# A hybrid decoder layer: input scales ahead of the pairs, the second pair's projections before the first pair's output, one-hots from bias columns

## The chip, the cores and the metric

The kernel runs on one core of one Trainium2 chip. The metric is device time in microseconds for one launch, the median of three runs. One execution was profiled; its rows are in a section below.

## The reference, cut to what matters

One layer on 1024 tokens of width 1024, in float32:

```python
h = x
h = h + _token_mixers(_rmsnorm(h, norm_mix), ...)     # attention heads and a conv module, then W_out
h = h + _peer(_rmsnorm(h, norm_ffn), ...)             # product-key retrieval over 128 * 128 experts
ple_gate = sigmoid(_rmsnorm(h, norm_ple) @ w_ple_gate)
h = h + ple_gate * (p @ w_ple_proj)
return _rmsnorm(h, final_norm)
```

`_rmsnorm` divides each token's row by the root of its mean square. The mixer projects the normed row to q, k, v and two conv inputs, runs three dilated causal windows over earlier tokens and a causal depthwise conv of 31 taps, and projects both through `w_out`. `_peer` finds for each token and each of 8 heads the 16 best of 128 * 128 experts, as pairs of the best 16 in two lists of 128 keys; an expert is one row of `expert_u` and one of `expert_v`: gelu(x . u) times a gate, times v.

## The kernel before, in words

The 1024 tokens are 8 tiles of 128, taken in four pairs (`GROUPS`; pair 0 holds tiles 0 and 1). Each pair passes through stages: `stage_in` (L823: load x, norm, transpose, projections q, k, v), `stage_attend` (L827: attention of the two tiles, then `convolve`), `stage_out` (L832: norms of both halves, `w_out`, residual, norm for the experts), `stage_search` (L837: queries, scores, the best 16 per list), `stage_combine` (L840: the best 16 pairs, indices and gates). Below, in(1) is `stage_in` of pair 1, and so on. Attention of a pair needs keys and values of the pairs before.

The experts are computed in two ways. For tiles 0, 1, 6, 7 (`FEW`) each of the 128 chosen rows of a token is fetched: `gather_all` (L623) walks these tiles one after the other, per tile 128 fetches of `expert_u` (GpSimd issues an indirect DMA, L592, for one slot of 128 tokens, 512 KB) each with a product and sum on VectorE (L605), then 128 fetches of `expert_v` with a multiply-add on VectorE (L621): 1024 fetches in all. For tiles 2 to 5 (`ALL`) all experts are computed: `gate_matrix` (L633) writes a matrix of gates per token and expert to DRAM, and `dense` (L697) streams both tables past it on TensorE, in split precision (lines L733 to L735 and L764 to L766). A closing stage `embed` (L772) follows for every tile.

A framework puts the instructions in order when the kernel is built: it walks them with estimated costs, and on each engine the ready instruction that was emitted first goes next; `tc.high_priority()` lifts a block. The order on each engine is then fixed, and an instruction at the head of a queue that waits holds up all that is behind it. The fetches are emitted last. SyncE (SP) issues the plain loads, in an order fixed in the same way. Tiles with the same tag share a few buffers: `xn` (2: x of a pair, later normed rows), `t4` (2: attention scores, large temporaries of `combine`), `w` (3 weight pieces), `xT` (1).

Norm scales come from `rstd` (L140): a square with row sum on ScalarE per tile, a square root on ScalarE (L150), a reciprocal on VectorE (L152). `normed_input` (L281) calls it, rescales the rows in place on ScalarE (L285) and transposes them on TensorE (L161, `pt_mix`).

The conv runs 16 of its taps on ScalarE and GpSimd (L348, L349) and 15 on VectorE (L355); `cc` at L356 joins them.

`gate_matrix` works through groups of four slots, 32 per tile. For each it needs two one-hot matrices of 128 lines, one scaled by the gate (`oa`, VectorE, from `less_keys` of `i1`: two matmuls into `pd` that give index minus key), one plain (`o2`). Every second group makes `o2` on VectorE by a comparison (L668). The others make it on ScalarE from a second `less_keys` (L674, L675): 1 - |index - key|, cut at 0. Four products then fill `pG` (L678), and ScalarE copies it out (L679).

Of the kernel before, what the change touches and what calls it, by code (L numbers as in the profile page):

```python
# [10 lines left out]
F32 = mybir.dt.float32  # L11
# [4 lines left out]
AF = mybir.ActivationFunctionType  # L16
# [4 lines left out]
P = 128  # L21
D = 1024
# [3 lines left out]
GROUPS = ((0, 1), (2, 3), (4, 5), (6, 7))  # L26
NG = len(GROUPS)
# [74 lines left out]
def tile_layer(ctx, tc, t, consts, out):  # L102
    nc = tc.nc
    V, S, G = nc.vector, nc.scalar, nc.gpsimd

    x_d = t["x"][0]
# [10 lines left out]
    rows = lambda i: slice(i * P, (i + 1) * P)  # L117
    half = lambda f: slice(f * 512, (f + 1) * 512)

    def scope(parent, **kw):  # L120
        s = parent.enter_context(ExitStack())
        return s, s.enter_context(tc.tile_pool(bufs=1, **kw))

    cpool = ctx.enter_context(tc.tile_pool(name="cpool", bufs=1))
    small = ctx.enter_context(tc.tile_pool(name="small", bufs=2))
# [4 lines left out]
    mix, mpool = scope(ctx, name="mpool")  # L130
# [6 lines left out]
    acc = bank(ps_keep, "acc", 1)  # L137


    def rstd(srcs, n, name, junk=None, pool=small):  # L140

        ssq = pool.tile([P, len(srcs)], F32, tag="ssq", name=f"ssq_{name}", bufs=2)
        for j, src in enumerate(srcs):
            sq = junk(f"sqj_{name}_{j}") if junk else mpool.tile([P, D], BF16, tag="t2", name=f"sqj_{name}_{j}", bufs=3)
            S.activation(sq[:, :n], src, AF.Square, accum_out=ssq[:, j : j + 1])
        return inv_sqrt(ssq, 1.0 / n, name, pool)

    def inv_sqrt(v, scale, name, pool=small):
        sd = pool.tile([P, v.shape[1]], F32, tag="sd", name=f"sd_{name}", bufs=2)
        S.activation(sd, v, AF.Sqrt, bias=eps, scale=scale)  # L150
        r = pool.tile([P, v.shape[1]], F32, tag="r", name=f"r_{name}", bufs=4)
        V.reciprocal(r, sd)  # L152
        return r

    def transpose_to(dst, src, n, name, ps_tile, gain=None):

        for b in range(0, n, 4):
            m = min(4, n - b)
            pt = ps_tile(f"pt_{name}_{b}")
            for i in range(m):  # L160
                nc.tensor.transpose(pt[:, rows(i)], src[:, rows(b + i)], ident)  # L161
            if gain is None:
                S.copy(dst[:, b : b + m, :], pt[:, : m * P].rearrange("p (m c) -> p m c", c=P))
            else:
                for i in range(m):
                    S.activation(dst[:, b + i, :], pt[:, rows(i)], AF.Copy, scale=gain[:, b + i : b + i + 1])
# [5 lines left out]
    ident, iota = col(C_ID, P), col(C_IOTA, P)  # L172
# [12 lines left out]
    bias = apool.tile([P, SEQ], F32, name="bias")  # L185
# [87 lines left out]
    def load(g):  # L273
        xs = []
        for i in GROUPS[g]:
            xt = mpool.tile([P, D], F32, tag="xn", name=f"xt{i}", bufs=2)
            nc.sync.dma_start(xt, x_d[rows(i), :])
            xs.append(xt)
        return xs

    def normed_input(g, xs):  # L281
        r = rstd(xs, D, f"mix{g}")
        xT = apool.tile([P, KD, GN], F32, tag="xT", name=f"xT{g}")[:, :, : len(xs) * P]
        for j in range(len(xs)):
            S.activation(xs[j], xs[j], AF.Copy, scale=r[:, j : j + 1])  # L285
            transpose_to(xT[:, :, rows(j)], xs[j], KD, f"mix{g}_{j}", tps, g_mix)
        return xT

# [12 lines left out]
    def qkv(g, xT):  # L301
        qT = apool.tile([P, GT, H // 2, P], F32, tag="qT", name=f"qT{g}", bufs=2)

        def done_k(j, a):
            i = GROUPS[g][j]
            k = apool.tile([P, DA], F32, tag="qk", name=f"k{i}")
            S.copy(k, a)
            rope(k, i)
            transpose_to(kT[:, :, rows(i)], k, H // 2, f"k{i}", tps)

        def done_q(j, a):
            i = GROUPS[g][j]
            q = apool.tile([P, DA], F32, tag="qk", name=f"q{i}")
            S.copy(q, a)
            rope(q, i)
            transpose_to(qT[:, j], q, H // 2, f"q{i}", tps)

        token_major(xT, w_qkv, 1, f"k{g}", done_k)
        token_major(xT, w_qkv, 0, f"q{g}", done_q)
        token_major(xT, w_qkv, 2, f"v{g}", lambda j, a: S.copy(vt[:, GROUPS[g][j], :], a))  # L320
        return qT
# [82 lines left out]
    def mixed(g, ys, cT):  # L404
# [13 lines left out]
        for j in range(nt):  # L418
# [5 lines left out]
            V.bn_aggr(mv[:, j, :], st)  # L424
            pcs.append(pc)
        r = inv_sqrt(mv[:, :, 1], 1.0, f"ln{g}")
        yc = []
        for j in range(nt):
# [204 lines left out]
    def gate_matrix(gp, j, i1, i2, gate):  # L633

        tr = []
        for what, src in (("i2", i2), ("g", gate)):
            f = flat(src)
            if what != "g":
                f32 = mpool.tile([P, SLOTS], F32, tag="t2", name=f"gl{what}{j}", bufs=3)
                S.copy(f32, f)  # L640
                f = f32
            pt = pps(f"pgt{what}{j}")
            nc.tensor.transpose(pt[:, 0:P], f, ident)
            d = gp.tile([P, P], F32, tag=f"{what}T", name=f"{what}T{j}", bufs=2)
            S.copy(d, pt[:, 0:P])
            tr.append(d)
        i2T, gT = tr
        four = [P, 4, NK]

        def less_keys(ix, t0, name):  # L650

            pd = lin(name).rearrange("p (t k) -> p t k", k=NK)
            nc.tensor.matmul(pd, flat(ix), ident16[:, t0 : t0 + 4].unsqueeze(2).to_broadcast(four), start=True, stop=False)
            nc.tensor.matmul(pd, ones16, minus16.to_broadcast([1, 4, NK]), start=False, stop=True)
            return pd

        for b in range(P // BT):
            stage = gp.tile([P, NK, BT], F32, tag="stage", name=f"stage{j}_{b}", bufs=2)
            for o in range(0, BT, 4):
                t0 = b * BT + o  # L660
                oa = gp.tile(four, F32, tag="oa", name=f"oa{j}_{t0}", bufs=2)
                V.scalar_tensor_tensor(
                    oa, less_keys(i1, t0, f"pd1_{j}_{t0}"), 0.0, gT[:, t0 : t0 + 4].unsqueeze(2).to_broadcast(four),
                    ALU.is_equal, ALU.mult,
                )
                o2 = gp.tile(four, F32, tag="o2", name=f"o2_{j}_{t0}", bufs=3)
                if o % 8 == 0:
                    V.tensor_tensor(  # L668
                        o2, i2T[:, t0 : t0 + 4].unsqueeze(2).to_broadcast(four),
                        iota.unsqueeze(1).to_broadcast(four), ALU.is_equal,  # L670
                    )
                else:

                    S.activation(o2, less_keys(i2, t0, f"pd2_{j}_{t0}"), AF.Abs)  # L674
                    S.activation(o2, o2, AF.Relu, bias=1.0, scale=-1.0)  # L675
                pg = sps(f"pG{j}_{t0}")
                for e in range(4):
                    nc.tensor.matmul(pg[:, rows(e)], o2[:, e, :], oa[:, e, :], start=True, stop=True)  # L678
                S.copy(stage[:, :, o : o + 4], pg.rearrange("p (t i) -> p i t", i=NK))  # L679
            nc.sync.dma_start(gd[j, :, :, b], stage.rearrange("p (q c) t -> p q (c t)", c=GROUP))  # L680
# [137 lines left out]
    xs = load(0)  # L818
    load_tables()
    fetched, wide, h1s = {}, {}, {}  # L820
    st = {}

    def stage_in(g):  # L823
        xT = normed_input(g, xs if g == 0 else load(g))
        st[g] = (qkv(g, xT), xT)

    def stage_attend(g):  # L827
        qT, xT = st[g]
        ys = attend(g, qT)
        st[g] = (ys, convolve(g, xT))  # L830

    def stage_out(g):  # L832
        yT = mixed(g, *st[g])
        h1s[g] = project(g, yT)
        st[g] = normed_ffn(g, h1s[g])

    def stage_search(g):  # L837
        st[g] = search(g, st[g])

    def stage_combine(g):  # L840
        vals, idxs = st[g]
        for j, i in enumerate(GROUPS[g]):
            if i in FEW:
                i1, i2, gate = combine(i, vals[j], idxs[j], gpool, NF)
                fetched[i] = (places(i, i1, i2), gate)
            else:
                wide[i] = combine(i, vals[j], idxs[j], mpool, ND)

    stage_in(0)
    stage_attend(0)  # L850
    for g in range(NG - 1):
        if g > 0:
            stage_in(g + 1)
        stage_out(g)
        stage_search(g)
        if g == 0:
            stage_in(g + 1)
        if g > 0:
            stage_attend(g + 1)
        stage_combine(g)  # L860
        if g == 0:
            stage_attend(g + 1)
# [5 lines left out]
    gph, gp = scope(ctx, name="gph", side="right")  # L868
# [10 lines left out]
    for j, i in enumerate(ALL):  # L879
        gate_matrix(gp, j, *wide[i])  # L880
# [91 lines left out]
```

## Time and profile before

| | us |
|---|---|
| median of three runs (3216.42 to 3229.95) | 3220.88 |
| profiled execution | 3223.85 |
| its span, first to last instruction | 3222.1 |
| TensorE busy in the span | 2791.2 (87%) |
| VectorE busy | 2604.3 (81%) |
| ScalarE busy | 1098.6 (34%) |
| GpSimd busy | 1535.3 (48%) |

All times in the rows are microseconds from the first instruction. PE is TensorE's matmul, PEld its weight load, DVE VectorE, ACT ScalarE, POOL GpSimd. A matmul's end in the trace is modelled, and matmuls are pipelined, so that their times overlap. L12 is line 12 of the kernel. The granted clock is the share of TensorE's full speed that it was given.

### The profile page before, as it was taken

To read this page: it belongs to the slowest core of one execution; us is meant where nothing else is said; L and a number is where in the kernel's file an instruction comes from. 1 tells how busy PE (TensorE), PEld (TensorE's weight loads), DVE (VectorE), ACT (ScalarE), POOL (GpSimd) and SP (SyncE) were. 2 spreads that over 40 slices of the span, in tenths; PEclk is the share of its full clock that TensorE was granted. 3 is DMA by queue.
4 is the path that set the end of the run, shared out by engine and by line. 5 is a ranking of instruction groups with operands and counts; after the bars stand their busy time and mean duration, and the time that the engine had idled before them with its cause. 6 is when DMAs were issued, how large, how long until landed. Compare 5 with 4: busy or idle time off the path is not lost. (4 is left out here: it accounts for less than half of the span.)

```text
span 3222.1 us, 36302 instructions
## 1 busy us (share of the span) xinstructions
PE 2791.2 (87%) x11839; PEld 2020.0 (63%) x11839; DVE 2604.3 (81%) x5147; ACT 1098.6 (34%) x1926; POOL 1535.3 (48%) x1268
## 2 busy tenths in 40 slices
PE   6688959958995859995999998999999989999998
PEld 3464625843673536663777775777777757777764
DVE  1728886997899898885888887888889878888974
ACT  2712543363245126663222223222222322232233
POOL 0501585455435512324555555565566555555651
PEclk9898978979997879998999999999999999999999
DMA  5154769718932937989999999999999999999982
GB/s 161 53 176 160 264 208 335 260 46 314 338 140 94 347 126 225 291 266 368 329 338 328 327 324 345 329 339 347 320 338 331 322 339 338 335 331 330 325 316 101
DMA packets 307984, 878.36 MB, mean 273 GB/s; under 512 B 27162, under 2 KB 94130, under 8 KB 307794
## 3 DMA queue, kind: packets, MB, share of 16 engines
q0 software_dynamic: 147456, 536.94, 46.2%
q1 hardware_dynamic: 157072, 335.74, 30.1%
q10 hardware_dynamic: 3266, 3.36, 0.3%
q8 instruction: 93, 1.52, 0.2%
q14 instruction: 97, 0.79, 0.1%
HBM read 833.99 MB, written 41.94 MB: 272 GB/s over the span
## 5 line engine op out<-in xcount | busy, mean ns | idle before, releaser
L592 POOL DMA_INDIRECT u<-in_expert_u_dram,ex x512 | 657.0, 1283 | 888.6 <-DVE hk L605 547.0
L592 POOL DMA_INDIRECT v<-in_expert_v_dram,ex x512 | 683.1, 1334 | 546.9 <-DVE gy L621 405.8
L621 DVE SCALAR_TENSOR_TENSOR gy<-v,ga,gy 128x1024 f32<-128x1024 f32 x512 | 656.8, 1283 | 58.7 <-DMA v<-in_expert_v_dram,ex 50.3
L605 DVE CUSTOM_DVE_ANT_0 u<-u,gxn 128x1024 f32<-128x1024 f32 x512 | 616.4, 1232 | 36.5 <-DMA u<-in_expert_u_dram,ex 36.3
L735 PE MATMUL ph<-xh,ul 128*128 128x512 f32 x1024 | 411.1, 401 | 37.7 <-DVE ul L711 37.6
L734 PE MATMUL ph<-xl,uh 128*128 128x512 f32 x1024 | 408.8, 399 | 0.0
L733 PE MATMUL ph<-xh,uh 128*128 128x512 f32 x1024 | 408.2, 399 | 0.4 <-ACT gelu L737 0.2
L751 ACT CAST vh<-v 128x1024 fp32r<-128x1024 f32 x128 | 131.3, 1050 | 675.4 <-PE py L766 476.7
L764 PE MATMUL py<-vh,ah 128*128 128x512 f32 x640 | 255.1, 399 | 38.4 <-ACT ah L743 38.3
L349 POOL TENSOR_TENSOR side<-side,tap 128x256 f32<-128x256 f32 x240 | 195.0, 814 | 183.7 <-ACT tap L348 169.8
L735 PEld LDWEIGHTS ph<-xh,ul 128*128 128x128 f32 x1024 | 196.3, 192 | 91.8 <-DVE ul L711 48.9
L766 PE MATMUL py<-vh,al 128*128 128x512 f32 x640 | 251.2, 397 | 0.3 <-DVE al L745 0.3
L765 PE MATMUL py<-vl,ah 128*128 128x512 f32 x640 | 249.9, 394 | 0.0
L753 DVE TENSOR_TENSOR vl<-v,vh 128x1024 fp32r<-128x1024 f32 x128 | 155.5, 1220 | 108.7 <-ACT vh L751 105.4
L269 PE MATMUL pq<-x2T,w_pq 128*128 128x256 f32 x1024 | 231.4, 384 | 4.0 <-DMA w_pq<-in_peer_wq_dram 3.0
L733 PEld LDWEIGHTS ph<-xh,uh 128*128 128x128 f32 x1024 | 196.7, 192 | 45.2 <-ACT gelu L737 2.4
L734 PEld LDWEIGHTS ph<-xl,uh 128*128 128x128 f32 x1024 | 196.5, 192 | 44.5 <-issue 2.2
L269 PEld LDWEIGHTS pq<-x2T,w_pq 128*128 128x128 f32 x1024 | 194.6, 193 | 32.9 <-ACT pqT L479 4.5
L709 ACT CAST uh<-u 128x1024 fp32r<-128x1024 f32 x128 | 134.3, 1049 | 127.3 <-PE ph L734 84.2
L743 ACT CAST ah<-gelu 128x512 fp32r<-128x512 f32 x128 | 79.3, 619 | 274.7 <-DVE gelu L741 272.3
L711 DVE TENSOR_TENSOR ul<-u,uh 128x1024 fp32r<-128x1024 f32 x128 | 156.0, 1219 | 20.8 <-DMA gt<-gate_d 13.3
L764 PEld LDWEIGHTS py<-vh,ah 128*128 128x128 f32 x640 | 120.8, 189 | 76.1 <-ACT ah L743 50.2
(265 smaller groups left out, 4939.2 us busy)
## 6 DMA issues: line engine op xcount, KB each, us to landing
u<-in_uT_dram SPq DMA_DIRECT2D x128, 512.0 KB
v<-in_expert_v_dram SPq DMA_DIRECT2D x128, 512.0 KB
w_pq<-in_peer_wq_dram SPq DMA_DIRECT2D x64, 512.0 KB
gate_d<-stage SPq DMA_DIRECT2D x16, 2048.0 KB
gt<-gate_d SPq DMA_DIRECT2D x64, 512.0 KB
w_o<-in_w_out_dram SPq DMA_DIRECT2D x32, 512.0 KB
we<-in_w_ple_gate_dram SPq DMA_DIRECT2D x24, 512.0 KB
w_k<-in_w_qkv_dram SPq DMA_DIRECT2D x16, 512.0 KB
```

Of the source, the lines that this page charges most:

```text
L269: nc.tensor.matmul(a, w[:, k, :], xT[:, k, :], start=k == 0, stop=k == KD - 1)
L349: G.tensor_tensor(side, side, m, ALU.add)
L592: d = G.indirect_dma_start(out=e, out_offset=None, in_=table, in_offset=bass.IndirectOffsetOnAxis(ap=index, axis=0))
L605: uses(V.tensor_tensor_reduce(out=e, in0=e, in1=xn, scale=1.0, scalar=0.0, op0=ALU.mult, op1=ALU.add, accum_out=hk[:, k : k + 1]))
L621: uses(V.scalar_tensor_tensor(y, e, act[:, k : k + 1], y, ALU.mult, ALU.add))
L711: V.tensor_tensor(lo, u, hi.bitcast(F32), ALU.subtract)
L733: nc.tensor.matmul(ph, hi, xh[:, k, :], start=k == 0, stop=False)
L734: nc.tensor.matmul(ph, hi, xl[:, k, :], start=False, stop=False)
L735: nc.tensor.matmul(ph, lo, xh[:, k, :], start=False, stop=k == KD - 1)
L764: nc.tensor.matmul(py, ah[e][:, rows(j)], vh[e][:, half(f)], start=first, stop=False)
L765: nc.tensor.matmul(py, ah[e][:, rows(j)], vl[e][:, half(f)], start=False, stop=False)
L766: nc.tensor.matmul(py, al[e][:, rows(j)], vh[e][:, half(f)], start=False, stop=last_e)
```

## The change

Three edits. The scales of all pairs are worked out ahead (`input_scales`): those of pair 0 first, those of pairs 1 to 3 behind `stage_attend(0)` in `later_scales`, which loads x once more, into `t4` buffers, two tiles at a time. `normed_input` only rescales. Then in(1) is emitted ahead of out(0) and search(0) instead of behind them; the later pairs had that order already. Last, the groups of `gate_matrix` that make `o2` on ScalarE no longer use `less_keys`: ScalarE takes the absolute value of the key numbers with the negated index as a bias column, four slots in four instructions; `i2N` holds the negated indices of a tile.

```diff
-        return inv_sqrt(ssq, 1.0 / n, name, pool)
+        return inv_sqrt(ssq, 1.0 / n, name, pool, r_tag)
...
+    def input_scales(g, xs):
+        r = rstd(xs, D, f"mix{g}", r_tag="r_mix")
+        for j, i in enumerate(GROUPS[g]):
+            r_mix[i] = r[:, j : j + 1]
+
+    def later_scales():
+        for g in range(1, NG):
+            xs = []
+            for i in GROUPS[g]:
+                xt = mpool.tile([P, D], F32, tag="t4", name=f"xq{i}", bufs=2)
+                nc.sync.dma_start(xt, x_d[rows(i), :])
+                xs.append(xt)
+            input_scales(g, xs)
...
     def normed_input(g, xs):
-        r = rstd(xs, D, f"mix{g}")
...
-            S.activation(xs[j], xs[j], AF.Copy, scale=r[:, j : j + 1])
+            S.activation(xs[j], xs[j], AF.Copy, scale=r_mix[GROUPS[g][j]])
...
+        i2N = gp.tile([P, P], F32, tag="i2N", name=f"i2N{j}", bufs=2)
+        S.activation(i2N, i2T, AF.Copy, scale=-1.0)
...
-                    S.activation(o2, less_keys(i2, t0, f"pd2_{j}_{t0}"), AF.Abs)
+                    for e in range(4):
+                        S.activation(o2[:, e, :], iota, AF.Abs, bias=i2N[:, t0 + e : t0 + e + 1])
                     S.activation(o2, o2, AF.Relu, bias=1.0, scale=-1.0)
...
+    input_scales(0, xs)
     stage_in(0)
     stage_attend(0)
+    later_scales()
     for g in range(NG - 1):
-        if g > 0:
-            stage_in(g + 1)
+        stage_in(g + 1)
         stage_out(g)
         stage_search(g)
-        if g == 0:
-            stage_in(g + 1)
         if g > 0:
             stage_attend(g + 1)
         stage_combine(g)
```

## Rows read from the trace of the kernel before

**Rows 1.** Stretches: length; PE, PEld, DVE, ACT, POOL busy (count); clock; DMA share; GB/s.

```profile
298.00:489.00 191.00, 147.56 (x531) 83.58 (x530) 166.42 (x365) 78.24 (x168) 128.64 (x125) 0.87 0.71 242
...
1196.00:1460.00 264.00, 252.30 (x1436) 158.72 (x1436) 221.50 (x361) 154.10 (x274) 69.88 (x65) 0.97 0.81 253
...
1440.00:1520.00 80.00, 48.15 (x175) 28.44 (x175) 45.70 (x75) 23.07 (x39) 34.18 (x28) 0.83 0.99 358
...
1491.00:3107.00 1616.00, 1500.04 (x6287) 1189.88 (x6286) 1373.20 (x1807) 442.57 (x582) 912.17 (x667) 0.98 0.92 332
3107.00:3222.00 115.00, 98.61 (x290) 48.90 (x288) 62.14 (x69) 40.56 (x90) 30.04 (x26) 0.95 0.48 181
```

**Rows 2.** The same for the gathers of line L592 alone: POOL busy (x).

```profile
298.00:489.00 191.00, 79.30 (x65) 0.87 0.71 242
```

**Rows 3.** Timeline of the tail: start, us, engine, line, operation [idle before, releaser].

```profile
3146.26 1.02 POOL L592 DMA_INDIRECT v<-in_expert_v_dram,ex  x1 [0.30 <-issue]
...
3159.22 2.60 DVE L621 SCALAR_TENSOR_TENSOR gy<-v,ga,gy 128x1024 f32<-128x1024 f32 x2
...
3209.25 2.74 PE L804 MATMUL plp<-wt,pTt 128*128 128x512 f32 x6
```

**Rows 4.** Timeline: the first matmul of the dense product, and its last.

```profile
1491.16 0.79 PE L733 MATMUL ph<-xh,uh 128*128 128x512 f32 x1
...
3107.01 0.39 PE L766 MATMUL py<-vh,al 128*128 128x512 f32 x1
```

**Rows 5.** Timeline of PE: the first transposes of pairs 1, 2 and 3.

```profile
275.76 1.11 PE L161 MATMUL pt_mix<-cst,xt 128*128 128x128 f32 x4 [9.56 <-ACT xt L285]
...
424.71 1.12 PE L161 MATMUL pt_mix<-cst,xt 128*128 128x128 f32 x4 [28.37 <-ACT xt L285]
...
722.57 1.12 PE L161 MATMUL pt_mix<-cst,xt 128*128 128x128 f32 x4 [35.72 <-ACT xt L285]
```

**Rows 6.** Pair 2's root and reciprocal; both gaps per stretch.

```profile
409.37 0.29 ACT L150 ACTIVATE sd_mix<-ssq_mix,eps 128x2 f32<-128x2 f32 x1
...
423.32 0.15 DVE L152 RECIPROCAL r_mix<-sd_mix 128x2 f32<-128x2 f32 x1
...
396.00:424.60 28.60, 0.34 (x2) 0.00 (x0) 28.60 (x49) 17.54 (x38) 19.33 (x24) 0.59 0.11 37
...
687.00:722.50 35.50, 0.00 (x0) 0.00 (x0) 35.50 (x56) 19.11 (x40) 19.72 (x25) 0.56 0.04 15
```

**Rows 7.** Around the moved stage: a stretch, then timeline of pairs 1 and 2.

```profile
121.00:201.00 80.00, 45.63 (x104) 20.60 (x105) 37.97 (x61) 35.95 (x79) 25.25 (x33) 0.74 0.28 93
...
331.00 0.38 DVE L549 TENSOR_TENSOR i<-eq 128x128 bf16<-128x128 bf16 x1
...
332.52 0.92 PE L374 MATMUL s<-kT,qT 64*128 64x384 f32 x4
...
373.57 0.89 ACT L348 ACTIVATE tap<-glu,cw 128x256 f32<-128x256 f32 x2
...
471.97 0.41 DVE L356 TENSOR_TENSOR cc<-cc,side 128x256 f32<-128x256 f32 x1
...
489.28 1.04 PE L421 MATMUL pc<-cst,cc 128*128 128x128 f32 x8
...
715.11 0.41 DVE L356 TENSOR_TENSOR cc<-cc,side 128x256 f32<-128x256 f32 x1
```

**Rows 8.** Gate matrices: two `pd` matmuls; small ScalarE operations elsewhere; the `Abs`.

```profile
1228.09 0.38 PE L653 MATMUL pd<-ident,i 128*128 128x512 bf16 x1
1228.40 0.38 PE L654 MATMUL pd<-minus,ones 1*128 1x512 bf16 x1
...
36.02 1.15 ACT L166 ACTIVATE xT<-pt_mix,gains 128x128 f32<-128x128 f32 x4 [1.01 <-PE pt_mix L161]
...
77.31 0.40 ACT L384 ACTIVATE sb<-sb,nm 128x128 f32<-128x128 f32 x1
...
L674 ACT ACTIVATE o<-pd 128x512 f32<-128x512 f32 x64 | 38.3, 598 | 17.1 <-PE pd L654 16.4 <-DVE o L668 0.7
```

More of the change, by code (lines that the diff above doesn't have):

```diff
@@ L137, in tile_layer, with rstd @@
     acc = bank(ps_keep, "acc", 1)
-    def rstd(srcs, n, name, junk=None, pool=small):
+    def rstd(srcs, n, name, junk=None, pool=small, r_tag="r"):
         ssq = pool.tile([P, len(srcs)], F32, tag="ssq", name=f"ssq_{name}", bufs=2)
@@ L145, in rstd, with inv_sqrt @@
             S.activation(sq[:, :n], src, AF.Square, accum_out=ssq[:, j : j + 1])
-        return inv_sqrt(ssq, 1.0 / n, name, pool)
-    def inv_sqrt(v, scale, name, pool=small):
+        return inv_sqrt(ssq, 1.0 / n, name, pool, r_tag)
+    def inv_sqrt(v, scale, name, pool=small, r_tag="r"):
         sd = pool.tile([P, v.shape[1]], F32, tag="sd", name=f"sd_{name}", bufs=2)
         S.activation(sd, v, AF.Sqrt, bias=eps, scale=scale)
-        r = pool.tile([P, v.shape[1]], F32, tag="r", name=f"r_{name}", bufs=4)
+        r = pool.tile([P, v.shape[1]], F32, tag=r_tag, name=f"r_{name}", bufs=4)
         V.reciprocal(r, sd)
@@ L820, in tile_layer @@
     fetched, wide, h1s = {}, {}, {}
-    st = {}
+    st, r_mix = {}, {}
     def stage_in(g):
```

## The prediction

> **What bounds the kernel now.** I read the stage table first (busy time of each engine in chosen stretches), because no engine is the bound all the way. Between 1491 and 3107 us (first `ph` to last `py` matmul [rows 4]) TensorE works on the dense experts: 1500 of 1616 us busy, DMA share 0.92 at 332 GB/s [rows 1]. This stretch is not touched by the diff and I let it keep its length. Then 115 us of tail follow [rows 1]. Second view: the same table for the row gathers of GpSimd (`fetch`, L592). Of 1024 rows 65 are issued in 298 to 489 us [rows 2]. Beside the dense product and in the tail GpSimd does nothing else, so its counts in the stage table are rows too: 667 and 26 [rows 1]; 331 lie before. A row goes out every 1616/667 = 2.42 us beside the dense product, every 1.32 us behind it (1.02 of issue and 0.30 to the next [rows 3]). The last row is added at 3161.8 us, 54.8 us behind the last `py` [rows 3, 4].
>
> So two things set the end together. The dense product must start early, and the gathers must be through. They are emitted last, so they only fill the free slots of VectorE and GpSimd; a shorter front leaves them fewer. Third view: TensorE's order of work ahead of 1491, for its idle times and what ended them; there the change acts.
>
> **How an edit moves the end.** If the dense product starts D us earlier and L rows fewer are issued before it, the dense product ends at 3107 - D, the tail of TensorE at 3107 - D + 115. The gathers end at 3107 - D + 54.8 + 1.35 L (1.32 us of spacing, a little for VectorE's own tail work). Behind the last row its tile still needs about 37 us: 5 for the norm, 21 for TensorE (transposes, two halves of 8.6), 11 from the last `plp` (at 3211) to the end [rows 3]. So end = 3107 - D + max(115, 92 + 1.35 L); up to 17 lost rows cost nothing, later ones 1.35 us each. The price of a row has 2.42 us as its upper end (dense pace to the finish) and 0 as its lower (it finds another free slot); I take 1.35, since lost rows run after the last `py`, where that pace is measured.
>
> **Scales first.** Today `stage_in` of pairs 2 and 3 starts with two squares, a square root, a reciprocal on VectorE, a rescale. TensorE waits 28.4 us before the first `pt_mix` of pair 2, 35.7 before that of pair 3, 9.6 before that of pair 1 [rows 5]. The wait isn't the arithmetic: for pair 2 the root is done at 409.7 and its reciprocal, 0.15 us long, runs at 423.3, behind convolution work in VectorE's queue [rows 6]. With scales worked out during pair 0 this wait goes; the rows of x are in their buffers by then, so the rescale on ScalarE is late next, a few us. The granted clock averages 0.59 and 0.56 over the two gaps [rows 6], near the lower of its two levels; what an earlier return to the upper one saves I count as nothing. What isn't gained: VectorE is busy 28.6 of 28.6 and 35.5 of 35.5 us in the two gaps [rows 6]. If `out` of the same pair then waits for VectorE's convolution, the projections are only early. When in(2) is through, out(1) begins at 489.3, 17 us behind the last `cc` of pair 1 at 472.4 [rows 7]; so of the 28.4 us 17 come even if VectorE's work stays where it is (they are in the 65 below). For pair 3 the last `cc` of pair 2 is ready at 715.5 [rows 7], before in(3) even starts; so VectorE holds out(2) only through the rotations of in(3), which wait in its full queue. I count 25 of 35.7, bounds 0 and 36.
>
> Added: six loads of x, 512 KB each, into the two `t4` buffers; the squares and roots only move. Between 121 and 201 us the DMA share is 0.28 [rows 7], so 3 MB, 9 us at the 332 GB/s of rows 1, are hidden. On SP each load after the second waits for a square to free its buffer, and weight pieces of the convolution and of in(1) stand behind it; three pieces fetched ahead cover that. ScalarE is busy 36 of these 80 us. Six squares of about 1.1 us and a table load cost it about 9, which can push taps, and through them the convolution of pair 0: 0 to 9 us, I take 4. The reciprocal of pair 1 still stands behind that convolution on VectorE, 13.6 us at worst if it goes as for pair 2 [rows 6].
>
> **Order of pair 1.** in(1) leaves 275.8 to 332.5 us, 56.8 us [rows 5, 7], and is put on TensorE behind the convolution's matmuls of pair 0. There TensorE is busy 45.6 of 80 us [rows 7], so 34 us are free and the moved work doesn't fit: out(0) and search(0) come later by 56.8 - 34 = 23 us at most; at least by 0, if the waits inside in(1) take out(0)'s matmuls. I take 12, which holds the 4 above. Queued behind that are combine(0) and the first gather, 298 becomes 310, 4 rows fewer at 65/191 = 0.34 a us. Then combine(0) has VectorE without anything beside it until 331.4 + 12 = 343 [rows 7], while attend(1) begins today at 332.5. So attend(1) does not start earlier. But its convolution matmuls and in(2) no longer queue behind in(1): TensorE is free from 277 on. The first tap, today 373.6, and with it the 99 us to the last `cc` at 472.4 [rows 7] can come 30 to 60 us sooner, and in(2), which fills TensorE's holes in attend(1), comes with the 28.4 us gap gone. For the start of out(1) I take 65 us earlier in all; bounds -6 (VectorE sets it) and 85 (all of in(1) and the gap).
>
> **One-hots.** For 64 groups of four slots the two `pd` matmuls go, 0.31 us apart [rows 8]: 64 x 2 x 0.31 = 40 us off TensorE, which is busy 252 of 264 us in this stage [rows 1]. ScalarE's `Abs` of 0.60 us over 512 columns becomes four of 128 with a bias column. No row shows that operation. The nearest are four copies of 128 columns with a scale column in 1.15 us, and the exponential of 128 columns with a bias column, 0.40 us alone [rows 8]; four cost 1.15 to 1.6 us. By 1.3, nearer to the row of four, this adds 64 x 0.7 = 45 us to ScalarE's 154 [rows 1]: 199 of 224 left, close to the bound. The `i2N` copy, once per tile, is nothing. I take 30 us, bounds 0 and 40.
>
> **Sum.** D = 65 + 25 + 30 = 120 (bounds -6 and 161). L = 120 x 0.34 + 4 = 45, at the rate of the richest stretch throughout; bounds 0 and 59. End = 3107 - 120 + 92 + 61 = 3140 of the span; the profiled run took 1.75 us more than its span (3223.85), and the median of the runs is 3 us below it. Together 3139 us, 2.5% less.
>
> **Rivals.**
> R1, the rows cost nothing: the gathers speed up beside the dense product, TensorE sets the end: 3107 - 120 + 115 - 1 = 3101. For it: idle times of VectorE there (243 us of 1616 [rows 1]). Against it: 0.92 of DMA time is taken, and where the share is 0.99 the chip moves 358 GB/s [rows 1], so little room is left. The Trainium skill (Perfetto Trace Analysis, Roofline) says that a core that is active alone can go past 358 GB/s up to what its 16 DMA engines carry together, about 435; by this, an estimate, the dense stretch had room for some 300 more rows, and 3101 would be it. The trace does not agree: 358 comes with the engines 99% busy.
> R2, VectorE sets the boundaries: the filled gaps were full for it, its work is the same, out(1) and out(3) hardly move, ScalarE eats the gate's gain. D = 10: 3107 - 10 + 115 - 1 = 3211.
> R3, slower: the place is 310 to 489 us. attend(1), its convolution and in(2) crowd there and take VectorE's and GpSimd's slots, while combine(0) at 343 keeps the boundary; D = 35, all 65 rows of that stretch lost: 3107 - 35 + 92 + 88 - 1 = 3251. It decides from L above (D + 23)/1.35, 43 rows here. For it: 65 rows in 191 us is where the front is richest. Against: what shortens the stretch must show in D.
> R4, ScalarE binds the gate matrices (1.6 us instead of 1.3, and waits): D = 90, L = 35: 3107 - 90 + 92 + 47 - 1 = 3155.
> That later scales do nothing is out: the reciprocal's wait is read, and its instruction leaves that queue.
>
> **How the numbers follow.** Forecast 0.50 (3139, own range 3122 to 3163 for D from 150 to 75), R1 0.14, R4 0.12, R2 0.14, R3 0.10. The range goes to 3070 (D of 150 with rows that cost nothing: 3071) and up to 3212, which takes in R2 and leaves R3 out. Under 0.5% (16 us, about what a measurement of this kernel can tell from no change) counts as the same: from 3205 to 3237. Faster: 0.50 + 0.14 + 0.12 and 0.02 of R2, 0.78. Same: 0.12. Slower: 0.10.
>
> **What would show it.** First `pt_mix` of pairs 2 and 3 without an idle time above 5 us before it. First gather near 310. out(1)'s `pc` near 424 instead of 489. Gate stage 225 to 245 us instead of 264, with ScalarE over 190 busy. First `ph` near 1371, dense product 1616 long, some 285 rows before it, some 70 after it. The forecast is wrong if `ph` starts later than 1440, or if the dense stretch gets longer by more than 20 us, or if more than 100 rows are left at its end.

## The result, and the profile after

The changed kernel takes 3254.69 us in the median (four runs, 3251.73 to 3256.99) against 3218.65 of the kernel before beside it: ratio 1.0097, 95% interval 1.0073 to 1.0121. It is 1% slower; 3139 us with a range of 3070 to 3212 was forecast. The profiled run took 3251.73 us, its span 3250.0.

Stretches of the changed kernel, columns as in [rows 1]: around the start of the gathers, the gate stage, the dense product, the tail.

```profile
342.00:489.00 147.00, 124.63 (x352) 71.09 (x353) 112.42 (x265) 65.36 (x150) 88.88 (x89) 0.69 0.38 136
1180.00:1409.00 229.00, 214.43 (x1310) 148.65 (x1310) 202.19 (x279) 187.74 (x463) 46.86 (x46) 0.95 0.80 243
...
1434.00:3060.40 1626.40, 1505.97 (x6320) 1188.81 (x6321) 1376.74 (x1883) 443.84 (x592) 915.66 (x673) 0.98 0.92 333
3060.40:3250.00 189.60, 101.01 (x288) 50.69 (x286) 144.59 (x135) 43.76 (x92) 106.18 (x92) 0.77 0.79 291
```

The first of these stretches again, with GpSimd's busy time in the gathers alone (line L605) and their count:

```profile
342.00:489.00 147.00, 35.47 (x29) 0.69 0.38 136
```

The timeline at the first gather, the edges of the dense product, and the end:

```profile
341.84 1.08 POOL L605 DMA_INDIRECT u<-in_expert_u_dram,ex  x1 [187.91 <-DVE ex L591]
...
1434.00 0.79 PE L749 MATMUL ph<-xh,uh 128*128 128x512 f32 x1 [25.29 <-ACT uh L725]
...
3059.99 0.39 PE L782 MATMUL py<-vh,al 128*128 128x512 f32 x1
...
3207.58 1.01 POOL L605 DMA_INDIRECT v<-in_expert_v_dram,ex  x1 [0.31 <-issue]
3210.02 5.31 DVE L634 SCALAR_TENSOR_TENSOR gy<-v,ga,gy 128x1024 f32<-128x1024 f32 x4 [0.33 <-DMA v<-in_expert_v_dram,ex]
3238.46 1.88 PE L820 MATMUL plp<-wt,pTt 128*128 128x512 f32 x4
```

Read them against [rows 1 to 4]. The dense product starts 57 us earlier and ends 47 us earlier (it is 10 us longer). But 92 rows are left behind it instead of 26, because only 259 instead of 331 were issued ahead of it: 29 up to 489 us instead of 65. The last row is added at 3215.3 us, 155 us behind the last `py` instead of 55. TensorE works only 101 of the last 190 us; it waits for rows.

What TensorE does at the boundaries of the pairs (timeline of PE; answers to [rows 5, 7]):

```profile
152.71 1.12 PE L161 MATMUL pt_mix<-cst,xt 128*128 128x128 f32 x4 [30.72 <-ACT xt L298]
...
361.30 5.78 PE L260 MATMUL k<-w_k,xT 128*128 128x512 f32 x6 [3.57 <-ACT xT L166]
...
445.73 7.03 PE L260 MATMUL k<-w_k,xT 128*128 128x512 f32 x16
...
489.73 1.04 PE L434 MATMUL pc<-cst,cc 128*128 128x128 f32 x8
...
701.85 0.60 PE L161 MATMUL pt_mix<-cst,xt 128*128 128x128 f32 x4
...
765.01 1.04 PE L434 MATMUL pc<-cst,cc 128*128 128x128 f32 x8
```

in(1) doesn't fill TensorE's holes in the convolution of pair 0: it waits 30.7 us and starts when that convolution is all but over (its last `cc` runs at 154.0 us). out(0), search(0), combine(0) and the first gather all come behind it, the gather 43.5 us later than before. And out(1) starts at 489.7 as before, since in(2), begun early, gets its last operands 84 us after its first. Between the two stands the attention of attend(1). Its stretch, from the first `s` to the last `po` matmul, in the changed kernel and in the one before (columns as above):

```profile
374.30:441.40 67.10, 62.36 (x201) 41.15 (x201) 39.30 (x91) 35.08 (x87) 26.02 (x32) 0.52 0.00 1
```

```profile
332.50:376.70 44.20, 44.20 (x242) 29.78 (x242) 34.62 (x79) 25.64 (x56) 21.21 (x22) 1.00 0.84 285
```

It takes 67 us instead of 44, at a granted clock of 0.52 (near the lower of the two levels, 1.2 GHz) instead of 1.00 (2.4 GHz). In the kernel before, the matmuls of in(1) run right up to it; in the changed one TensorE has waited 15.5 us up to 347.7 and several times more behind that. So it is TensorE's own order of work that holds out(1), not VectorE's convolution: pair 1's last `cc` is done at 466.3, 23 us ahead of out(1). No run changes the clock alone.

**VectorE's account.** Each row needs VectorE once, so the rows can be counted against its time. The next windows run from zero to the first `ph` (and to the first gather), for the kernel before and the changed one; behind each long one stand the same window for the lines of the u product and of the `gy` addition, whose first time is VectorE's.

```profile
0.00:1491.20 1491.20, 1192.75 (x5266) 781.29 (x5266) 1169.18 (x3273) 615.66 (x1255) 593.14 (x575) 0.89 0.63 215
...
0.00:1491.20 1491.20, 243.47 (x394) 0.89 0.63 215
...
0.00:1491.20 1491.20, 164.73 (x128) 0.89 0.63 215
...
0.00:298.30 298.30, 226.62 (x848) 146.48 (x849) 137.09 (x554) 112.89 (x259) 46.16 (x64) 0.90 0.40 128
```

```profile
0.00:1434.00 1434.00, 1174.53 (x5106) 790.27 (x5106) 1073.45 (x3131) 643.79 (x1439) 517.72 (x503) 0.88 0.58 199
...
0.00:1434.00 1434.00, 155.12 (x256) 0.88 0.58 199
...
0.00:1434.00 1434.00, 160.04 (x125) 0.88 0.58 199
...
0.00:341.80 341.80, 265.00 (x1023) 174.25 (x1023) 141.11 (x577) 126.21 (x283) 46.75 (x64) 0.93 0.44 143
```

Before: 1169.2 busy, of it 243.5 + 164.7 = 408.2 for 331 rows (1.23 us a row); 761.0 of other work; 322.0 idle. After: 315.2 for 259 rows; 758.3 of other work; 360.6 idle. The other work is the same. By this account a front that is shorter by D, with VectorE idle for as long as before, loses D/1.23 = 0.81 D rows. Here D is 57, and the idle time grew by 38.6 on top: by 39.5 ahead of the first gather, where VectorE has no rows to work on (298.3 - 137.1 = 161.2 us before, 341.8 - 141.1 = 200.7 after), by 10 from there to 489 us and 6 in the next stretch, while the shorter gate stage has 16 less. (57.2 + 38.6 - 2.7)/1.23 = 76 rows by this, 72 were lost.

This is bookkeeping: it adds up without saying why VectorE is idle, and one stretch shows that idle time alone brings no rows. The changed kernel fetches six rows, as many as there are buffers for them (`ge`), and then none for 86 us (GpSimd, VectorE twice, GpSimd):

```profile
353.62 1.23 POOL L605 DMA_INDIRECT u<-in_expert_u_dram,ex  x1
...
389.35 0.56 DVE L391 CUSTOM_DVE_ANT_0 sb<-s,bias 128x384 f32<-128x384 f32 x1 [2.33 <-PE pt_p L161]
...
436.63 1.22 DVE L618 CUSTOM_DVE_ANT_0 u<-u,gxn 128x1024 f32<-128x1024 f32 x1
...
441.03 0.95 POOL L605 DMA_INDIRECT u<-in_expert_u_dram,ex  x1
```

The first product with a row (L618), after which the seventh row is fetched, stands in VectorE's fixed order behind steps of attend(1) that wait for TensorE. VectorE is idle for 27.8 of the 67.1 us above and the DMA share is 0.00. In the five kernels with the new order the first product comes 83 to 95 us behind the first gather, in the eight with the old order 13 to 15. Of the 72 lost rows 36 belong up to 489 us (17 were issued there before 342, when the changed kernel has no indices yet, and 19 fewer follow), 13 to the middle, 23 to the gate stage, which is shorter.

### The profile page after: what moved, and what is told of

Same layout as the page of the kernel before. It is cut to its first block, busy times and chain, and to the rows that moved or that the text cites. A ratio compares the mean times of both kernels' runs of the same rounds, so it can differ in the third digit from the quotient of the medians.

```text
span 3250.0 us, 36215 instructions
## 1 busy us (share of the span) xinstructions
PE 2781.5 (86%) x11711; PEld 2029.8 (62%) x11711; DVE 2594.8 (80%) x5147; ACT 1131.4 (35%) x2123; POOL 1539.6 (47%) x1268
## 4 chain that ended last, share of the span: by engine, by line
PE 34%; DVE 22%; issue 17%; DMA 14%; POOL 9%; ACT 3%; SPq 0%; ACTq 0%; POOLq 0%; DVEq 0%
POOL v L605 5%; DMA v<-in_expert_v_dram 4%; PE pG L694 4%; DVE u L618 3%; PE plg L814 3%; DVE gy L634 3%; PE pq L269 3%; POOL u L605 2%; DMA u<-in_expert_u_dram,ex 2%; PE po L403 2%; DVE cc L368 2%; PE s L387 2%; DMA v<-in_expert_v_dram,ex 2%; DVE ul L727 2%; POOL side L362 2%
## 5 line engine op out<-in xcount | busy, mean ns | idle before, releaser
L605 POOL DMA_INDIRECT u<-in_expert_u_dram,ex x512 | 679.3, 1327 | 745.6 <-DVE hk L618 414.1
L605 POOL DMA_INDIRECT v<-in_expert_v_dram,ex x512 | 659.7, 1288 | 703.4 <-DVE gy L634 584.8
L618 DVE CUSTOM_DVE_ANT_0 u<-u,gxn 128x1024 f32<-128x1024 f32 x512 | 610.6, 1222 | 52.8 <-DMA u<-in_expert_u_dram,ex 49.0
```

The costliest lines, as they stand in the source:

```text
L605: d = G.indirect_dma_start(out=e, out_offset=None, in_=table, in_offset=bass.IndirectOffsetOnAxis(ap=index, axis=0))
L618: uses(V.tensor_tensor_reduce(out=e, in0=e, in1=xn, scale=1.0, scalar=0.0, op0=ALU.mult, op1=ALU.add, accum_out=hk[:, k : k + 1]))
```

## The experiments

All numbers of the trace are of the profiled run; "behind" is the rows issued after the last `py`, "idle" is VectorE's ahead of the first `ph`. A ratio is that of the medians, against runs of the kernel before beside it.

| kernel | first gather | first `ph` | rows before / in / behind | idle | span | ratio (95%) |
|---|---|---|---|---|---|---|
| before | 298 | 1491.2 | 331 / 667 / 26 | 322 | 3222.1 | 1 |
| changed | 342 | 1434.0 | 259 / 673 / 92 | 361 | 3250.0 | 1.0097 (1.0073-1.0121) |
| a1 one-hots only | 298 | 1452.0 | 311 / 666 / 47 | 307 | 3193.3 | 0.9910 (0.9889-0.9930) |
| a2 scales only | 295 | 1442.4 | 303 / 667 / 54 | 315 | 3188.3 | 0.9897 (0.9858-0.9936) |
| a3 order only | 334 | 1504.9 | 300 / 666 / 58 | 382 | 3257.1 | 1.0079 (1.0055-1.0102) |
| a4 scales and one-hots, old order | 294 | 1414.0 | 285 / 666 / 73 | 306 | 3194.0 | 0.9897 (0.9863-0.9932) |
| b1 changed, 40 rows left out | 339 | 1440.1 | 259 / 673 / 52 | 367 | 3203.8 | 0.9898 (0.9860-0.9937) |
| b2 changed, scales split | 338 | 1431.1 | 259 / 674 / 91 | 356 | 3246.0 | 1.0099 (1.0081-1.0118) |
| b3 a4 with 18 side taps | 302 | 1419.7 | 293 / 665 / 66 | 306 | 3179.9 | 0.9896 (0.9870-0.9921) |
| b4 a4 with 20 side taps | 308 | 1476.6 | 309 / 667 / 48 | 360 | 3209.3 | 0.9990 (0.9978-1.0002) |
| c1 a4, 40 rows left out | 294 | 1408.0 | 285 / 666 / 33 | 299 | 3149.8 | 0.9779 (0.9741-0.9816) |
| c2 changed, no side taps in pair 0 | 331 | 1397.9 | 251 / 674 / 99 | 327 | 3214.9 | 1.0006 (0.9984-1.0028) |
| c3 a4, 8 side taps in pair 0, else 18 | 299 | 1420.5 | 293 / 666 / 65 | 299 | 3186.0 | 0.9848 (0.9818-0.9879) |

**The three parts apart.** a1 is the kernel before with the one-hots' part of the diff; a2 with the scales' part; a3 with the order's part; a4 is the changed kernel with

```diff
     later_scales()
     for g in range(NG - 1):
-        stage_in(g + 1)
+        if g > 0:
+            stage_in(g + 1)
         stage_out(g)
         stage_search(g)
+        if g == 0:
+            stage_in(g + 1)
```

> The kernel before with ScalarE's one-hots from columns of biases and nothing else. Theory A (the new order of pair 1 costs the time; the one-hots earn what they promise): the gate stage becomes 30 to 37 us shorter, some 9 rows fewer are issued before the dense product, which stays under the 17 that are free, so the end falls by the same: 3180 to 3190 us, ratio about 0.99. Rival C (the longer ScalarE work of the gate stage takes the rows' slots and gives the gain back): D of 35 with 45 rows or more lost, 3219 us or above, ratio 1.00 or more.

> The kernel before with all input scales worked out first (later_scales behind the convolution of pair 0), pairs in the old order, old one-hots. Theory A: the idle times ahead of the projections of pairs 2 and 3 shrink, the first gather stays within 5 us of 298 us, the dense product starts 15 to 35 us earlier: 3190 to 3205 us, ratio 0.99 to 0.995. Rival B (the scales are what costs: six loads, squares and roots inside the convolution of pair 0 push out(0), search(0) and the first gather): first gather 15 us or more later, 3225 to 3250 us, ratio over 1.002.

> The kernel before with the second pair's projections emitted ahead of the first pair's output and nothing else. Theory A: out(0) and search(0) go behind in(1), the first gather comes 35 to 50 us later, out(1) starts no earlier than 489 us, the dense product starts no earlier than 1491 us with some 15 to 40 rows fewer before it: 3225 to 3270 us, ratio 1.002 to 1.015. Rival B (the order is good, the scales spoil it): out(1) starts 40 us or more earlier, 3165 to 3190 us, ratio under 0.99.

> The changed kernel with the second pair's projections put back behind the first pair's search; scales first and one-hots from biases stay. Theory A: first gather near 298 us, dense product 50 to 65 us earlier than before, 15 to 25 rows fewer before it, dense length 1616: end = 3107 - D + 92 + 1.35 L, 3155 to 3175 us, ratio 0.98 to 0.987, the best of all kernels so far. Rivals B and C: no better than the kernel before, ratio 0.997 or more.

Measured: the order costs 0.8%, each of the other two gains 1%, but both together gain no more than either; on top of both the order costs 2% (1.0097 against 0.9897). Rivals B and C fall. Theory A holds for the order (first gather 334, out(1) at 489.0). a1's 3196.12 us lies above its range, because 20 rows were lost, not 9; a2's 3192.30 lies within, with a dense product 49 us earlier instead of 15 to 35 and 28 rows lost. For a4 its time failed, 3197.21 us instead of 3155 to 3175, because 46 rows were lost, not 15 to 25. Its out(1) does come 29 us earlier than in [rows 7], its out(2) 35 us earlier (774.8 in the kernel before); a4, timeline of PE:

```profile
379.54 0.60 PE L161 MATMUL pt_mix<-cst,xt 128*128 128x128 f32 x4
...
460.04 1.04 PE L434 MATMUL pc<-cst,cc 128*128 128x128 f32 x8
...
739.34 1.04 PE L434 MATMUL pc<-cst,cc 128*128 128x128 f32 x8
```

Its dense product starts 28 us ahead of a2's, 18 rows fewer are before it, and the spans end within 6 us of each other. a1's gate stage, with ScalarE at 188 of 229 us:

```profile
1192.00:1421.00 229.00, 216.96 (x1319) 150.02 (x1318) 198.66 (x321) 188.42 (x469) 43.34 (x45) 0.94 0.80 244
```

**Are the rows what sets the end?** b1 and c1 are the changed kernel and a4 with

```diff
-        for k in range(SLOTS):
+        for k in range(SLOTS if i != FEW[-1] else SLOTS - 40):
             e = fetch(v_d, ex[:, k : k + 1], f"v{i}_{k}")
```

> The changed kernel without the last 40 of the 1024 row gathers (the last 40 of 128 rows of expert_v for the last tile, with their additions, are left out, so the last tile's output lacks them). Theory L (the time is the row gathers': what is left behind the dense product runs at 1.5 us a row, then 34 us follow): 92 rows left become 52, the end falls by 60 us, 3185 to 3200 us against 3250. Rival R1 (rows are hidden, TensorE's tail of 115 us behind the dense product sets the end): no change, 3245 to 3255 us. If a row were worth the 2.42 us it takes beside the dense product, the end would be TensorE's, 3176 us.

> The kernel with scales first and the new one-hots in the old order, without the last 40 of the 1024 row gathers (40 of 128 rows of expert_v for the last tile and their additions are left out, so that tile's output lacks them). Theory L (its dense product starts 77 us earlier than in the kernel before, and all of that beyond 28 us is lost to the 73 rows left behind it): with 33 rows left the gathers end near 3131 us, TensorE's tail near 3143, so 3140 to 3152 us, ratio 0.975 to 0.98. Rival (something else behind the dense product holds the end): 3185 us or more.

b1 takes 3197.03 us, c1 3149.52: both as theory L said. Their tails (stretch behind the last `py`; b1, then c1):

```profile
3071.20:3203.80 132.60, 100.19 (x289) 49.69 (x286) 93.19 (x95) 43.75 (x92) 61.37 (x52) 0.89 0.70 257
```

```profile
3035.60:3149.80 114.20, 98.32 (x289) 48.09 (x287) 69.76 (x74) 39.40 (x88) 39.13 (x33) 0.96 0.57 210
```

189.6 us of tail become 132.6 with 40 rows fewer, 1.43 us a row; c1's 114.2 is the 115 of [rows 1], TensorE's own. So a4's earlier dense product is worth its 77 us only once the rows are gone (72 us between c1's span and that of before). Over the profiled runs of all kernels with more than 43 rows behind, span = last `py` + 49.6 + 1.52 us a row, within 7 us (1.52 from 26 and 92 rows, 54.4 and 154.9 us to the last `gy`; 49.6 is what is left of the changed kernel's 189.6).

**Why in(1) does not start at 122 us.** In the changed kernel ScalarE has the roots of pair 1 and pair 3, and then pair 1's rescale, at

```profile
139.14 0.29 ACT L150 ACTIVATE sd_mix<-ssq_mix,eps 128x2 f32<-128x2 f32 x1
...
149.79 0.28 ACT L150 ACTIVATE sd_mix<-ssq_mix,eps 128x2 f32<-128x2 f32 x1
...
151.52 1.13 ACT L298 ACTIVATE xt<-xt,r_mix 128x1024 f32<-128x1024 f32 x1
```

so the rescale stands behind squares of pairs 2 and 3, whose first `pt_mix` comes 174 and 549 us later (326.5, 701.9). b2 takes those away, c2 the convolution's taps:

```diff
-    def later_scales():
-        for g in range(1, NG):
+    def later_scales(pairs):
+        for g in pairs:
...
     stage_in(0)
+    later_scales((1,))
     stage_attend(0)
-    later_scales()
...
         stage_search(g)
+        if g == 0:
+            later_scales((2, 3))
```

```diff
-SIDE_TAPS = 16
+SIDE_TAPS = (0, 16, 16, 16)
...
-        cT = []
+        cT, side_taps = [], SIDE_TAPS[g]
...
-            V.tensor_tensor(cc, cc, side, ALU.add)
+            if side_taps:
+                V.tensor_tensor(cc, cc, side, ALU.add)
```

> The changed kernel with the scales of pair 1 worked out ahead of attend(0) and those of pairs 2 and 3 behind search(0); order and one-hots as changed. Theory H (the 31 us in which TensorE waits before the first pt_mix of pair 1 come from the squares and reciprocals of pairs 2 and 3 and of pair 1 in the queues of ScalarE and VectorE): that wait falls under 10 us, in(1) starts near 125 us, the first gather comes 20 to 28 us earlier (314 to 322 us), 10 to 20 rows more stand before the dense product, 3215 to 3235 us. Rival T (the convolution's taps of pair 0 hold both queues whatever is added): in(1) starts at 142 us or later as in the kernel with the order alone, 3240 to 3255 us.

> The changed kernel with all 31 taps of pair 0's convolution on VectorE (64 tap products fewer on ScalarE, 60 additions fewer on GpSimd, 64 taps more on VectorE in that one stage). Theory T2 (in the new order the projections of pair 1 are held by ScalarE, whose rescale and gain copies for them stand between taps that wait for GpSimd): in(1) is through by 185 us instead of 202, the first gather comes 14 to 24 us earlier (318 to 328 us), 10 to 20 rows more before the dense product, 3215 to 3235 us. Rival V (VectorE takes over as what holds out(0)): the convolution of pair 0 ends at 175 us or later, in(1) may be early, the first gather comes at 340 us or later, 3245 to 3265 us.

b2, timeline of PE:

```profile
120.72 3.62 PE L269 MATMUL a<-xT,w_a 128*128 128x256 f32 x16
124.17 0.60 PE L161 MATMUL pt_mix<-cst,xt 128*128 128x128 f32 x4
...
140.47 2.08 PE L260 MATMUL k<-w_k,xT 128*128 128x512 f32 x2 [15.70 <-ACT xT L166]
```

The first `pt_mix` comes at 124 us, as H said, and nothing is won: the gain copies behind it stand among ScalarE's taps, and in(1) is through at 197.6 instead of 201.9. In c2 there are no such taps; now the reciprocals stand behind the convolution on VectorE (ScalarE's root of pair 1, VectorE, then pair 1's rescale):

```profile
120.81 0.29 ACT L150 ACTIVATE sd_mix<-ssq_mix,eps 128x2 f32<-128x2 f32 x1
...
133.78 7.22 DVE L368 SCALAR_TENSOR_TENSOR cc<-glu,cw,cc 128x256 f32<-128x256 f32 x18
140.91 0.23 DVE L152 RECIPROCAL r_mix<-sd_mix 128x2 f32<-128x2 f32 x2
...
141.37 2.17 ACT L298 ACTIVATE xt<-xt,r_mix 128x1024 f32<-128x1024 f32 x2
```

in(1) ends at 191.0, the gather starts at 331: 11 us earlier, T2's numbers are missed, and 8 rows fewer, not 10 to 20 more, stand before the dense product. That its time, 3223.75 us, lies in T2's range is luck: out(1) comes at 465.0, and the dense product starts 36 us earlier than in the changed kernel. Whichever single obstacle goes, pair 0's convolution holds in(1) by the next queue; that all of them together would let it run from 122 was not tried. What c2 shows by the way is the account at its plainest: the dense product starts 93 us ahead of the kernel before, 99 rows are behind it, the time is the same (ratio 1.0006).

**Work off VectorE.** b3, b4 and c3 change `SIDE_TAPS` of a4, to 18, 20 and (8, 18, 18, 18).

> The kernel with scales first and the new one-hots in the old order, and 18 instead of 16 of the 31 taps on ScalarE and GpSimd (32 fewer tap operations of 0.73 us on VectorE, 32 more of 0.5 us on ScalarE and 0.86 us on GpSimd). Theory L (VectorE's work before the dense product sets how many rows it gets through there): VectorE's other work there falls by 12 to 23 us, 10 to 18 rows more are issued before the dense product, end 15 to 27 us earlier than the same kernel with 16 taps: 3167 to 3182 us. Rival G (ScalarE and GpSimd set the convolution): out(1), out(2) and out(3) come later, the dense product starts 10 us later or more, 3195 to 3215 us.

> The same with 20 taps on ScalarE and GpSimd (64 fewer on VectorE). Theory L alone: 25 to 46 us less work on VectorE, 20 to 37 rows more, bounded by TensorE's tail 115 us behind the dense product: 3143 to 3170 us. Rival G: the convolutions of pairs 1 to 3 get up to a quarter longer, dense product 20 to 40 us later, 3200 to 3230 us.

> Scales first, new one-hots, old order, with 8 taps on ScalarE and GpSimd for pair 0 (23 on VectorE, which has no rows to work on yet) and 18 for the other pairs. Theory L (VectorE's time before the first gather is worth nothing, so it should do more there and less later): pair 0's convolution ends 5 to 12 us earlier than its 153 to 159 us, the first gather comes at 285 to 295 us, some 5 to 12 rows more before the dense product than with 18 taps everywhere: 3165 to 3180 us. Rival V: VectorE alone holds that convolution, which ends at 160 us or later; 3185 to 3200 us.

b3 issues 8 rows more ahead of the dense product (10 to 18 were expected), its profiled span is 14 us shorter than a4's, but over the runs the two ratios are equal (0.9896 and 0.9897): inconclusive. In b4 rival G holds: out(1)'s last `pc` waits for the taps until 510 us and the idle time grows to 360. c3 has the best time of the kernels that fetch all rows, 3174.93 us, in its range, though not for the reason given: gather at 299 instead of 285 to 295, the same 293 rows as b3 (its profiled run, 3187.86 us, is the longest of its four). Its interval meets b3's and a4's; against the kernel before it is 1.5% faster, against the changed one's 1.0097 some 2.5%.

## Why the prediction was wrong

The formula for the end held: with the measured D = 57 and L = 72 it gives 3107 - 57 + 92 + 97 = 3239 of a span of 3250, and 10 of the missing 11 us are the longer dense product. What fed it failed, in two steps. What came is nearest to R3, which had a chance of 0.10: it comes in the place that R3 named (29 rows instead of 65 up to 489 us), with 72 rows against its threshold of (57 + 23)/1.35 = 59. R3's mechanism holds only in part: attend(1) didn't fill VectorE, which was idle for 27.8 of 67.1 us there; the rows' work stood behind it in a fixed order.

- *Order of pair 1, "65 us earlier in all"*: wrong in sign. TensorE's 34 free us beside the convolution of pair 0 were counted as room for in(1); b2 and c2 show that in(1)'s own ScalarE and VectorE work stands in those engines' queues with that convolution. out(0) came behind all of in(1): the first gather moved by 43.5 us, not 12. out(1) gained nothing; against a4's 460.0 it lost 30. attend(1), which the forecast let start no earlier, started 42 us later, and its attention took 23 us longer, at the granted clock of 0.52. R2's unmoved out(1) came too, but from TensorE and not from VectorE.
- *Rows lost, "at the rate of the richest stretch"*, 0.34 a us: wrong kind of rate. By VectorE's account an edit that cuts the front and leaves VectorE's other work and idle time alone takes 0.81 rows per us, less the idle time that goes with it. Measured: 20 of 39 us in a1, 28 of 49 in a2, 46 of 77 in a4, 72 of 57 here, where idle time was added and the rows stopped for 86 us. Had D = 120 come with a4's 0.60, L would have been 72 and the forecast 3176.
- *Price of a row, 1.35 us*: 1.52 between 26 and 92 rows, 1.43 in b1. The 17 free rows stand: 43 behind is where TensorE's 115 us and the rows' 49.6 + 1.52 a row meet, and there were 26.
- *R1*: the dense product took 665 to 674 rows in every kernel, whether 251 or 331 had gone before. The gathers didn't speed up. Whether the DMA engines (share 0.92) or the fixed order holds them to that number, no run shows. The Trainium skill (Perfetto Trace Analysis, Roofline) gives a core that is active alone a practical ceiling of about 435 GB/s; this stretch moves 333.
- *Scales first*: right in the sum. a2's dense product starts 49 us earlier (28.4 + 25 were taken). out(1) comes 28 us earlier, out(2) 35, so pair 3's gap gave 7 there instead of 25; the rest comes behind out(2).
- *One-hots*: right, a little low. The gate stage takes 229 us instead of 264, ScalarE is busy 188; a1's dense product starts 39 us earlier (30 were taken). R4 didn't come.

## What to carry to other kernels

Where a background stream fills the free slots of one engine, write that engine's account first: stretch = fixed work + idle + stream. In these runs cutting another engine's stall took slots from the stream, and a gain was left where the cut removed the filler engine's own idle time or where lost slots were still free at the end. The stream uses idle time only where the fixed order lets it: look for stretches in which both the filler engine and the stream stand still. Free time of one engine is no room for a stage whose operands come through other engines' in-order queues: look there for what stands ahead.

## What the runs showed of the hardware

A tap on VectorE takes twice as long while GpSimd adds. Pair 0's convolution in the changed kernel, with GpSimd adding beside it, and in c2, without:

```profile
112.24 10.51 DVE L368 SCALAR_TENSOR_TENSOR cc<-glu,cw,cc 128x256 f32<-128x256 f32 x12
```

```profile
108.08 6.02 DVE L368 SCALAR_TENSOR_TENSOR cc<-glu,cw,cc 128x256 f32<-128x256 f32 x15
```

0.88 us against 0.40 us each. The Trainium skill (SBUF — State Buffer, Who interferes with whom) says that a VectorE instruction with two inputs in SBUF contends with a GpSimd instruction that reads SBUF; the rows agree. So 16 taps given to ScalarE and GpSimd relieve VectorE of less than they seem to: with 64 taps more, c2's VectorE is busy 145.0 us ahead of the first gather, against 141.1.
